# RMSNorm with every row written twice: gamma by three DMAs and one broadcast, the second load as two transfers

## The chip, the cores and the metric

The kernel runs on one core of a Trainium2 chip. The metric is device time in microseconds (us) for one execution; lower is better. The time of the kernel before is the median of three executions. The profile is one execution, recorded by the hardware profiler. In it ACT is the scalar engine, DVE the vector engine, POOL the GpSimd engine, SP the engine that issues most DMAs, and PE the matmul engine, which this kernel doesn't use.

## The reference

```python
B, S, D = 8, 512, 2048                       # x: (8, 512, 2048) float32, gamma: (2048,) float32

def reference(x, gamma):
    x_rep = np.repeat(x, 2, axis=1)
    rms = np.sqrt((x_rep ** 2).mean(axis=-1, keepdims=True) + 1e-6)
    return (x_rep / rms * gamma[None, None, :]).astype(np.float32)   # (8, 1024, 2048)
```

Each of the 4096 rows of x is divided by its root mean square, multiplied by gamma, and written twice in a row. 33.55 MB are read and 67.11 MB are written.

## The kernel before, in words

**Tiling.** The 4096 rows are taken in four loads of 1024. In one load every one of the 128 partitions gets 8 consecutive rows, 64 KB that lie together in memory. Each row is written twice, so a load makes two stores of the same size: 4 rows a partition, doubled, are 64 KB again. All the data stays in one buffer `y` of 24 rows a partition, which is used as three regions of 8 rows (L47, `first`, `second`, `third`).

**Stages.** `four(n, constants)` handles two loads, `n` and `n + 1`, and is called twice. Load `n` goes to rows 4 to 11, load `n + 1` to the region `third` (rows 16 to 23). For each group of 4 rows:

- `squares` runs on ACT: one pass a row (L63), which squares it and adds it up, and then the root of all rows of the group (L67).
- `scale` runs on DVE: the reciprocal of the roots (L73), then for each row one instruction (L75) that multiplies by it and by `gamma_b`, which has gamma in every partition.
- `repeat` copies each scaled row beside itself, on ACT or DVE (L82).
- `store` is one DMA from SP (L53).

In `four` the stores come in the order `first`, `second`, `first` again, `third`; call them store 1 to 4 of a call. The scaling for store 3 writes where store 1 reads, so it waits for store 1 to have landed.

**Order.** `manual_schedule` is on: every engine runs its instructions in the order in which the program writes them. All loads (L50) and stores (L53) are issued by SP, and so share one DMA queue, q1 in the profile. Gamma's DMAs are issued by ACT, on queue q10. SP issues both loads of a call first; then it waits in turn for what each store needs. The loads of the second call wait for stores of the first that read the same rows.

**Gamma.** `constants` is called once, between the two first loads. Gamma's first 2000 elements go as 16 pieces of 125 (500 B) into partition 0 of rows 0 and 1 of `y` (L121), with a gap after each piece; the other 48 go as three DMAs of 16 elements (64 B) into partition 0 of row 2 (L127). `y` is free there until the first scaling. Then POOL copies partition 0 to all 128 partitions of `gamma_b`, in two instructions: the 2000 elements (L131) once the first DMA has landed, and the 48 (L135) once the three have. After its DMA issues ACT loads its function table and takes one root that nothing uses (L139).

The helper that builds the program (`kernel`) is the same in both. Lines L157 and L168 of the profile belong to it.

Of the kernel before, what the change touches and what calls it, by code (L numbers as in the profile page):

```python
# [1 line left out]

# [4 lines left out]


@with_exitstack
def kernel(  # L10
    ctx: ExitStack,
    tc: tile.TileContext,
    x: bass.AP,
    gamma: bass.AP,
    out: bass.AP,
):
    nc = tc.nc
    P = nc.NUM_PARTITIONS
    f32 = mybir.dt.float32
    Act = mybir.ActivationFunctionType  # L20
    Alu = mybir.AluOpType

    B, S, D = x.shape
    Bo, So, Do = out.shape
    R = So // S
    assert R == 2 and D == Do and B == Bo and So == S * R
    eps = 1e-6
    inv_d = 1.0 / float(D)


    K = 4
    N = B * S
    ntiles = N // (P * K)
    assert N % (P * K) == 0 and ntiles == 8
    H = 2
    x_t = x.rearrange("b s d -> (b s) d").rearrange("(n p k) d -> n p k d", p=P, k=H * K)
    out_t = out.rearrange("b s d -> (b s) d").rearrange("(n p h j) d -> n h p (j d)", p=P, h=H, j=K * R)

    singles = ctx.enter_context(tc.tile_pool(name="singles", bufs=1))
    rows = ctx.enter_context(tc.tile_pool(name="rows", bufs=1))  # L40
    junk = ctx.enter_context(tc.tile_pool(name="junk", bufs=1, space=bass.MemoryType.PSUM))
    small = ctx.enter_context(tc.tile_pool(name="small", bufs=4))

    y = rows.tile([P, 3 * K * R, D], f32, name="y")
    first, second, third = 0, K * R, 2 * K * R  # L47

    def load(n, at):
        nc.sync.dma_start(out=y[:, at : at + H * K, :], in_=x_t[n])  # L50

    def store(n, h, to):
        nc.sync.dma_start(  # L53
            out=out_t[n, h], in_=y[:, to : to + K * R, :].rearrange("p j d -> p (j d)")
        )

    def squares(at, rows):

        n = len(rows)
        ss = small.tile([P, n], f32, name=f"ss{n}")  # L60
        for c, k in enumerate(rows):
            sq = junk.tile([P, D], f32, name="sq")
            nc.scalar.activation(  # L63
                out=sq[:], in_=y[:, at + k, :], func=Act.Square, accum_out=ss[:, c : c + 1]
            )
        rms = small.tile([P, n], f32, name=f"rms{n}")
        nc.scalar.activation(out=rms[:], in_=ss[:], func=Act.Sqrt, scale=inv_d, bias=eps_t[:])  # L67
        return rms

    def scale(at, to, rows, rms):  # L70
        n = len(rows)
        rstd = small.tile([P, n], f32, name=f"rstd{n}")
        nc.vector.reciprocal(out=rstd[:], in_=rms[:])  # L73
        for c, k in enumerate(rows):
            nc.vector.scalar_tensor_tensor(  # L75
                out=y[:, to + R * k, :], in0=y[:, at + k, :], scalar=rstd[:, c : c + 1],
                in1=gamma_b[:], op0=Alu.mult, op1=Alu.mult,
            )

    def repeat(to, k0, k1, copy):  # L80
        y_r = y[:, to + R * k0 : to + R * k1, :].rearrange("p (k r) d -> p k r d", r=R)
        copy(out=y_r[:, :, 1, :], in_=y_r[:, :, 0, :])  # L82

    ctx.enter_context(tc.manual_schedule())

    half = K // 2
    up, down = list(range(K)), list(range(K - 1, -1, -1))

    def four(n, constants):


        load(n, first + K)
        constants()
        load(n + 1, third)
        for rows in (up[:half], up[half:]):
            scale(first + K, first, rows, squares(first + K, rows))
        repeat(first, 0, half, nc.scalar.copy)
        repeat(first, half, K, nc.vector.tensor_copy)
        store(n, 0, first)
        scale(second, second, down, squares(second, down))  # L100
        repeat(second, half, K, nc.scalar.copy)
        repeat(second, 0, half, nc.vector.tensor_copy)
        store(n, 1, second)
        roots = [squares(third + h * K, up) for h in range(H)]
        scale(third, first, up, roots[0])
        repeat(first, 0, half, nc.scalar.copy)
        repeat(first, half, K, nc.scalar.copy)
        store(n + 1, 0, first)
        scale(third + K, third, up, roots[1])
        repeat(third, 0, K, nc.scalar.copy)  # L110
        store(n + 1, 1, third)

    gamma_b = singles.tile([P, D], f32, name="gamma_b")
    G, E = 16, 3
    C = D // G - E
    gamma_s = y[0:1, 0:2, :].rearrange("p k (c d) -> p (k c) d", c=G // 2)
    gamma_t = y[0:1, 2, :]
    eps_t = singles.tile([P, 1], f32, name="eps_t")

    def constants():  # L120
        nc.scalar.dma_start(  # L121
            out=gamma_s[0:1, :, :C],
            in_=gamma[: G * C].rearrange("(p c d) -> p c d", p=1, c=G),
        )
        for c in range(E):
            at = G * C + c * G
            nc.scalar.dma_start(  # L127
                out=gamma_t[0:1, c * G : (c + 1) * G],
                in_=gamma[at : at + G].partition_broadcast(1),
            )  # L130
        nc.gpsimd.partition_broadcast(  # L131
            out_ap=gamma_b[:, : G * C].rearrange("p (c d) -> p c d", c=G),
            in_ap=gamma_s[0:1, :, :C],
        )
        nc.gpsimd.partition_broadcast(out_ap=gamma_b[:, G * C :], in_ap=gamma_t[0:1, : E * G])  # L135
        nc.vector.memset(eps_t, eps)  # L136

        root = singles.tile([P, 1], f32, name="root")[:]
        nc.scalar.activation(out=root, in_=eps_t[:], func=Act.Sqrt)  # L139

    four(0, constants)
    four(2, lambda: None)


# [1 line left out]
_INS = ['x', 'gamma']  # L146
_OUTS = [((8, 1024, 2048), 'float32')]


# [23 lines left out]
```

## Time and profile before

| | us |
|---|---|
| time, median of 3 | 238.84 (238.44 to 238.92) |
| time of the profiled execution | 238.52 |
| span in that execution, first to last instruction | 236.3 |
| DVE busy | 84.4 |
| ACT busy | 110.2 |
| POOL busy | 2.8 |
| ACT waiting for loads, in total (2 waits) | 70.4 |
| the first load, from issue to landing | 22.0 |

The profiled execution's own time is 0.3 us under the median. It is 2.2 us longer than its span: that part lies outside the program's first and last instruction.

A row of the timeline gives the start and the length in us, the engine, the line, the operation, what it writes and reads, and in brackets how long the engine stood idle before it and what released it. An engine's name with a q (SPq, ACTq) is its sequencer, issuing a DMA: its length there is that of the issue, not of the transfer. In the page's part on DMA queues, each queue has its packets, the MB that they moved, and the time that they took as a share of 16 DMA engines over the whole span.

### The profile page before, as it was taken

Reading aid. Unit: us, or ns where it says so; the run is one execution under the profiler, and the core shown is the slowest. Engines: PE = TensorE matmul, PEld = TensorE weight load, DVE = VectorE, ACT = ScalarE, POOL = GpSimd, SP = SyncE. Lnnn points to the kernel's source line nnn. Section 1 sums busy time; section 2 is a strip of 40 time slices with the busy share of each in tenths; the row PEclk is TensorE's granted clock in tenths of the full one; section 3 lists DMA queues with packets and bytes.
Section 4 is the critical chain, followed back from the end, with each engine's and each line's share of the span. In section 5 each row is a group of like instructions: output and inputs, shape, how many; then the busy total and the mean of one; then the engine's idle time right before and its main releaser. Section 6 shows DMA issues by size and latency. Waiting matters only on the chain.

```text
span 236.3 us, 225 instructions
## 1 busy us (share of the span) xinstructions
DVE 84.4 (36%) x47; ACT 110.2 (47%) x86; POOL 2.8 (1%) x6
## 2 busy tenths in 40 slices
DVE  0000396594699500000000007929919992000000
ACT  2001989479998470000000049991999957400000
POOL 0110000000000000000000000000000000000000
DMA  9898989989898989999898988989898988989894
GB/s 355 356 532 355 521 366 466 422 388 499 355 532 356 521 366 466 422 399 488 355 532 355 510 377 377 510 355 532 355 532 355 510 377 388 499 355 532 355 532 177
DMA packets 1767, 100.68 MB, mean 426 GB/s; under 512 B 230, under 2 KB 230, under 8 KB 230
## 3 DMA queue, kind: packets, MB, share of 16 engines
q1 hardware_dynamic: 1728, 100.66, 98.7%
q10 hardware_dynamic: 38, 0.01, 0.0%
q14 instruction: 1, 0.01, 0.0%
HBM read 33.56 MB, written 67.11 MB: 426 GB/s over the span
## 4 chain that ended last, share of the span: by engine, by line
DMA 45%; ACT 26%; DVE 12%; issue 2%; DVEq 0%
DMA y<-in_x_dram 26%; DMA out_dram<-y 19%; ACT sq L63 15%; DVE y L75 12%; ACT y L82 11%; ACT rms L67 1%; DVE rstd L73 0%; DVEq L75 0%
## 5 line engine op out<-in xcount | busy, mean ns | idle before, releaser
L63 ACT ACTIVATE sq<-y 128x2048 f32<-128x2048 f32 x32 | 60.1, 1878 | 71.1 <-DMA y<-in_x_dram 70.4
L75 DVE SCALAR_TENSOR_TENSOR y<-y,rstd,gamma_b 128x2048 f32<-128x2048 f32 x32 | 73.8, 2348 | 1.6 <-DMA out_dram<-y 1.0
L82 ACT COPY y<-y 128x4096 f32<-128x4096 f32 (+1 forms) x10 | 42.6, 4283 | 19.1 <-DVE y L75 18.3
L73 DVE RECIPROCAL rstd<-rms 128x4 f32<-128x4 f32 (+1 forms) x10 | 1.7, 170 | 109.2 <-ACT rms L67 109.2
L82 DVE COPY y<-y 128x4096 f32<-128x4096 f32 x4 | 9.2, 2294 | 0.1
L63 ACT ACTIVATION_READ_ACCUMULATOR sq<-y 128x1 f32 x32 | 6.0, 186 | 0.0
L67 ACT ACTIVATE rms<-ss,eps_t 128x4 f32<-128x4 f32 (+1 forms) x10 | 3.0, 297 | 0.3
L139 ACT ACT_TABLE_LOAD x1 | 1.3, 1283 | 2.6 <-issue 2.6
L131 POOL PARTITION_BROADCAST gamma_b<-y x1 | 2.2, 2243 | 10.2 <-DMA y<-in_gamma_dram 10.2
L135 POOL PARTITION_BROADCAST gamma_b<-y x1 | 0.3, 323 | 10.2 <-DMA y<-in_gamma_dram 10.2
L136 DVE MEMSET eps_t<- 128x1 f32 x1 | 0.1, 59 | 0.8 <-PEq L157 0.8
L139 ACT ACTIVATE root<-eps_t 128x1 f32<-128x1 f32 x1 | 0.2, 202 | 0.0
L157 POOL MEMSET const-bfloat16-1.0<- 128x1 bf16 x1 | 0.1, 101 | 0.0
L157 POOL MEMSET const-uint8-127<- 128x1 uint8 x1 | 0.1, 101 | 0.0
L157 POOL MEMSET const-float32-0.0<- 128x1 f32 x1 | 0.1, 98 | 0.2 <-issue 0.2
L157 POOL MEMSET const-float32-1.0<- 128x1 f32 x1 | 0.1, 99 | 0.0
## 6 DMA issues: line engine op xcount, KB each, us to landing
out_dram<-y SPq DMA_DIRECT2D x8, 24.7
y<-in_x_dram SPq DMA_DIRECT2D x4, 31.4
y<-in_gamma_dram ACTq DMA_DIRECT2D x3, 0.1 KB
y<-in_gamma_dram ACTq DMA_DIRECT2D x1, 7.8 KB, 9.9
```

The costliest lines, as they stand in the source:

```text
L63: nc.scalar.activation(out=sq[:], in_=y[:, at + k, :], func=Act.Square, accum_out=ss[:, c : c + 1])
L67: nc.scalar.activation(out=rms[:], in_=ss[:], func=Act.Sqrt, scale=inv_d, bias=eps_t[:])
L73: nc.vector.reciprocal(out=rstd[:], in_=rms[:])
L75: nc.vector.scalar_tensor_tensor(out=y[:, to + R * k, :], in0=y[:, at + k, :], scalar=rstd[:, c : c + 1], in1=gamma_b[:], op0=Alu.mult, op ...
L82: copy(out=y_r[:, :, 1, :], in_=y_r[:, :, 0, :])
L131: nc.gpsimd.partition_broadcast(out_ap=gamma_b[:, : G * C].rearrange("p (c d) -> p c d", c=G), in_ap=gamma_s[0:1, :, :C],)
L135: nc.gpsimd.partition_broadcast(out_ap=gamma_b[:, G * C :], in_ap=gamma_t[0:1, : E * G])
L136: nc.vector.memset(eps_t, eps)
L139: nc.scalar.activation(out=root, in_=eps_t[:], func=Act.Sqrt)
L157: nc = _bacc.Bacc("TRN2", target_bir_lowering=False, num_devices=1)
```

## The change

The new `constants` loads gamma straight into partition 0 of `gamma_b`, by three DMAs from ACT. Each takes 16 pieces, one from each block of 128 elements: columns 0 to 47, 48 to 87, and 88 to 127 of every block, so pieces of 192, 160 and 160 B. One broadcast by POOL then copies partition 0 of `gamma_b` to all of its partitions, once all three have landed. The areas of `y` that held gamma are no longer used for it.

`load` can now cut a transfer by partitions. In the first call of `four` the second load becomes two DMAs on SP, partitions 0 to 63 and 64 to 127, each of 4.19 MB. The three other loads stay whole. The root is the same instruction with another way to name its tile.

```diff
-    def load(n, at):
-        nc.sync.dma_start(out=y[:, at : at + H * K, :], in_=x_t[n])
+    def load(n, at, parts=(0, P)):
+        for p0, p1 in zip(parts, parts[1:]):
+            nc.sync.dma_start(out=y[p0:p1, at : at + H * K, :], in_=x_t[n, p0:p1])
...
-    def four(n, constants):
+    def four(n, constants, ahead=(0, P)):
 
 
         load(n, first + K)
         constants()
-        load(n + 1, third)
+        load(n + 1, third, ahead)
...
-    G, E = 16, 3
-    C = D // G - E
-    gamma_s = y[0:1, 0:2, :].rearrange("p k (c d) -> p (k c) d", c=G // 2)
-    gamma_t = y[0:1, 2, :]
     eps_t = singles.tile([P, 1], f32, name="eps_t")
 
     def constants():
-        nc.scalar.dma_start(
-            out=gamma_s[0:1, :, :C],
-            in_=gamma[: G * C].rearrange("(p c d) -> p c d", p=1, c=G),
-        )
-        for c in range(E):
-            at = G * C + c * G
-            nc.scalar.dma_start(
-                out=gamma_t[0:1, c * G : (c + 1) * G],
-                in_=gamma[at : at + G].partition_broadcast(1),
-            )
-        nc.gpsimd.partition_broadcast(
-            out_ap=gamma_b[:, : G * C].rearrange("p (c d) -> p c d", c=G),
-            in_ap=gamma_s[0:1, :, :C],
-        )
-        nc.gpsimd.partition_broadcast(out_ap=gamma_b[:, G * C :], in_ap=gamma_t[0:1, : E * G])
+        G = 16
+        g_in = gamma.rearrange("(p c d) -> p c d", p=1, c=G)
+        g_to = gamma_b[0:1, :].rearrange("p (c d) -> p c d", c=G)
+        for c0, c1 in ((0, 48), (48, 88), (88, D // G)):
+            nc.scalar.dma_start(out=g_to[:, :, c0:c1], in_=g_in[:, :, c0:c1])
+        nc.gpsimd.partition_broadcast(out_ap=gamma_b[:], in_ap=gamma_b[0:1, :])
         nc.vector.memset(eps_t, eps)
...
-    four(0, constants)
+    four(0, constants, ahead=(0, P // 2, P))
     four(2, lambda: None)
```

Every instruction behind the edits stands one line further down until `constants`: what was L50, L53, L63, L67, L73, L75 and L82 is L51, L54, L64, L68, L74, L76 and L83. Gamma's DMAs are L122, its broadcast L123, the table load and the root L127.

More of the change, by code (lines that the diff above doesn't have):

```diff
@@ L113 @@
     gamma_b = singles.tile([P, D], f32, name="gamma_b")
-    G, E = 16, 3
-    C = D // G - E
-    gamma_s = y[0:1, 0:2, :].rearrange("p k (c d) -> p (k c) d", c=G // 2)
-    gamma_t = y[0:1, 2, :]
     eps_t = singles.tile([P, 1], f32, name="eps_t")
     def constants():
-        nc.scalar.dma_start(
-            out=gamma_s[0:1, :, :C],
-            in_=gamma[: G * C].rearrange("(p c d) -> p c d", p=1, c=G),
-        )
-        for c in range(E):
-            at = G * C + c * G
-            nc.scalar.dma_start(
-                out=gamma_t[0:1, c * G : (c + 1) * G],
-                in_=gamma[at : at + G].partition_broadcast(1),
-            )
-        nc.gpsimd.partition_broadcast(
-            out_ap=gamma_b[:, : G * C].rearrange("p (c d) -> p c d", c=G),
-            in_ap=gamma_s[0:1, :, :C],
-        )
-        nc.gpsimd.partition_broadcast(out_ap=gamma_b[:, G * C :], in_ap=gamma_t[0:1, : E * G])
+        G = 16
[4 more added lines that the diff above has]
+        nc.gpsimd.partition_broadcast(out_ap=gamma_b[:], in_ap=gamma_b[0:1, :])
         nc.vector.memset(eps_t, eps)
-        root = singles.tile([P, 1], f32, name="root")[:]
-        nc.scalar.activation(out=root, in_=eps_t[:], func=Act.Sqrt)
-    four(0, constants)
+        root = singles.tile([P, 1], f32, name="root")
+        nc.scalar.activation(out=root[:], in_=eps_t[:], func=Act.Sqrt)
+    four(0, constants, ahead=(0, P // 2, P))
     four(2, lambda: None)
```

## The prediction

> **What bounds the kernel now.** The page comes first: the slices, the transfer counts, the queues.
>
> ```profile
> span 236.3 us, 225 instructions
> DVE 84.4 (36%) x47; ACT 110.2 (47%) x86; POOL 2.8 (1%) x6
> ...
> DMA  9898989989898989999898988989898988989894
> ...
> q1 hardware_dynamic: 1728, 100.66, 98.7%
> q10 hardware_dynamic: 38, 0.01, 0.0%
> ```
>
> No compute engine is busy for half of the span, while the 16 DMA engines never drop under 8 tenths before the last slice. Queue q1 holds SP's four loads and eight stores; its packets alone fill 98.7% of 16 engines' span. So the kernel ends when that queue has drained.
>
> A packet's price: 12 transfers of 128 rows of 64 KB are 1536 data packets, and 16 completions each are 192 more, which gives the 1728. So 0.987 x 236.3 x 16 / 1536 = 2.43 us for 64 KB on one engine. A transfer puts 8 packets on each engine: 8 x 2.43 = 19.4 us, and twelve are 233 of the 236.3 us.
>
> Next the windows, to see whether a load is priced like a store (columns: window, length, busy of DVE, ACT, POOL, PEclk, DMA share, GB/s).
>
> ```profile
> 43.00:117.00 74.00, 30.33 (x16) 35.02 (x25) 0.00 (x0) 1.00 1.02 439
> 121.00:156.00 35.00, 11.85 (x7) 16.37 (x16) 0.00 (x0) 1.00 1.04 449
> ```
>
> The first window holds stores alone, the second loads alone. Both are full, at one rate within the rounding of 64 KB packets to a window's edges. All of this traffic spans 128 partitions.
>
> Last the timeline and the waits around gamma and the first store.
>
> ```profile
> 0.72 0.86 SPq L50 DMA_DIRECT2D y<-in_x_dram  x2
> ...
> 10.67 2.24 POOL L131 PARTITION_BROADCAST gamma_b<-y  x1 [10.25 <-DMA y<-in_gamma_dram]
> ...
> 23.07 0.32 POOL L135 PARTITION_BROADCAST gamma_b<-y  x1 [10.15 <-DMA y<-in_gamma_dram]
> ...
> 27.38 4.61 DVE L75 SCALAR_TENSOR_TENSOR y<-y,rstd,gamma_b 128x2048 f32<-128x2048 f32 x2
> ...
> 39.24 0.35 SPq L53 DMA_DIRECT2D out_dram<-y  x1
> ```
>
> gamma_b is whole at 23.07 + 0.32 = 23.39 us, 4.0 us before its first use; that use waits for the roots of the first load, not for gamma. The first store is issued at 39.24, when the second load (issued at about 1.2; 40.9 is the longest landing of a load) still has until about 42.1. Even the tightest hand-over leaves the queue covered, by 2.9 us.
>
> **The change, part by part.**
>
> *Gamma's issues on ACT.* Before, four took 0.59 + 1.21 = 1.8 us; now three, between 0.21 and 0.67 us each by the same rows, so 0.6 to 2.0. The table load and the root behind them end at 4.08 now, and ACT then waits for the first load until 22.72. That 18.64 us wait hides it: 0. Without that cover it would cost at most 0.2.
>
> *Gamma's packets.* q10's 38 are the 16 pieces of L121 and one 64 B piece of each L127 issue, each with a completion: 2 x (16 + 3). Three DMAs of 16 pieces make 96. The trace's packet records have 26 ns for 500 B and 9 ns for a completion: an engine had 35 ns, three of them (or one, three times) the 64 B pieces besides; now it has at most 3 x (26 + 9) = 105. These lie in the queue's own time: +0.07 us, bounds 0 and 0.2.
>
> *Gamma's landing and the broadcast.* The first DMA landed at 10.67, three more by 23.07, or 4.1 us apiece; two more land between 18.9 and 23.07. One broadcast is 2.24 x 2048/2000 = 2.3 us and, as POOL now waits for all three, it ends between 21.2 and 25.4. The first L75 needs it at 27.38, so at least 2.0 us are left; nothing else stands on POOL. Cost 0. Were it late by more than 2.0 + 2.9 us, store 1 would miss the queue's end.
>
> *The extra SP issue.* 0.34 to 0.43 us at about 1.6; SP next stands waiting until 39.24, and the queue holds two loads by then: 0. One completion more per engine: 0.01. ACT's squares of the second load now wait for two landings; they stand behind other work until 52.42, so a landing before that costs nothing. Behind them on ACT are only this pair's own squares and copies.
>
> *The second load itself, 128 partitions becoming 64 and 64.* This is the whole question. The pieces of L121 went to one partition and still made 16 packets, so engines are dealt out by pieces and not by partition: each half should run on all 16 engines, four packets apiece, the second half behind the first. No row shows a large transfer into 64 partitions.
> - Lower bound: each engine keeps its 2.43 us a packet. Then 4 x 2.43 twice is 19.4, as before: +0.
> - Upper bound: each partition keeps the most it is ever seen to take in. The whole is 8.39 MB in 19.4 us, 432 GB/s, or 3.4 GB/s a partition. 64 partitions then take 216 GB/s, each half 4.19 MB needs 19.4 us, and both 38.8: +19.4.
>
> What the edit halves is the number of partitions within reach at a time, so the rate per partition is the nearer row: no row has any part of the SBUF taking in more, while the lower bound asks double of it. I take +19.4.
>
> [...]
>
> *What is late next.* The load then lands at 42.1 + 19.4 = 61.5, and ACT's squares of it, at 52.42 now, wait 9 us; their first root, at 60.55 + 0.30, comes near 70. Store 1 stands behind the load on the same queue and lands near 80.8 instead of just before 61.48, where the L75 that waited for it starts. That L75, which overwrites what store 1 reads, then starts at 80.8: four of them (9.14) and the last copy of two (3.6) have store 3 issued near 93.6, and the queue reaches it, two stores of 19.4 after 61.5, at about 100. So neither delay sets the end. As the queue has no idle time to give up, nothing is won back later.
>
> *Sum.* The profiled execution took 238.52 us (span 236.3 and 2.2 around it); 238.52 + 19.4 + 0.07 + 0.01 = 258.0. It lay 0.3 under the median of 238.84, which the range covers.
>
> **The rivals.**
>
> *Half the partitions take the full rate.* Then everything but 0.1 us is hidden: 238.9. For it: every packet of the profile has one price, loads and stores alike, as if the engines alone set the rate. Against it: nothing in the profile ever put 16 engines on 64 partitions.
>
> *The halves overlap in part.* If engines drift apart, some are in the second half while others still fill the first, and both sides of the SBUF are in use. With half of the collision gone: +9.7, so 248.3. Against it: the slices show the engines in step (8 and 9 tenths throughout), and step is what makes them collide.
>
> *Faster, by the engine that ends last.* The three 64 B DMAs made one packet each, so they may all have sat on one engine and delayed it. q10's share rounds to 0.0%, below 0.05% of 16 x 236.3 us: at most 1.9 us. If all of that was on one engine, if that engine ended last, and if the halves keep the full rate, spreading gamma evenly gives up to 1.9 us back: 236.9 at best, 237.9 with half of it. It decides once the second load costs under 1 us. Against it: the records price such packets at some 10 ns.
>
> *The split is no split*, because the engines are dealt by partition after all, 8 for each half: then the halves run side by side and the time is that of the first rival.
>
> **How the numbers follow.** The forecast, 258.0, gets 0.66. Its own range is 255.5 to 260.6: one packet's overlap where the halves meet (2.43) below, and above it a fresh start for the second half, 22.0 us of the first load's landing less 19.4, so 2.6. Partial overlap 0.10, no loss 0.12 (the fourth rival within it), faster 0.12. Holding 8 in 10 needs the forecast, partial overlap and most of no loss: 238.5 to 260.6. A measurement of this kernel can tell about 0.2%, 0.48 us, from no change: faster 0.12, same 0.11, slower 0.77.
>
> **What would show it.** Queue counts of 13 x 16 + 1536 = 1744 and 96 confirm the packets. Right: the slices between 22 and 61 us move about half the GB/s at an unchanged busy share; store 1 lands near 80; ACT's wait for loads grows by about 9 us, and DVE's for stores from 1.0 to some 11; the mean falls to 394 GB/s. Wrong: five loads land with the second whole at about 42, and the span is within 1 us. gamma is wrong if its broadcast ends after 25.4, or if a DVE wait on POOL appears.

## The result, and the profile after

| | before | after |
|---|---|---|
| time, median of 5 runs each, us | 238.45 | 259.46 (259.19 to 259.65) |
| ratio to before | | 1.0871 (95%: 1.0856 to 1.0887) |
| span of the profiled execution, us | 236.3 | 257.5 |

The change costs 21.0 us; the forecast was 258.0, with 255.5 to 260.6 as its own range. The page of the changed kernel, in the lines that answer to those shown of before:

```profile
span 257.5 us, 224 instructions
DVE 84.4 (33%) x47; ACT 110.4 (43%) x86; POOL 2.5 (1%) x5
...
DMA  8979997895998998998998998998998998998995
GB/s 326 490 336 316 285 204 163 173 295 193 479 458 367 479 458 367 479 458 367 479 458 367 479 448 367 489 449 367 489 448 367 489 438 377 489 428 387 489 428 224
...
q1 hardware_dynamic: 1744, 100.66, 98.8%
q10 hardware_dynamic: 96, 0.01, 0.0%
```

DVE and ACT do the same work in the same time (DVE 84.4 us in both kernels, ACT 110.2 and 110.4), and queue q1 is as full as before: 98.8% beside 98.7%, of a longer span. The two digit rows have to be read against each other. From the fifth to the tenth slice (a slice is 257.5 / 40 = 6.4 us, so from 26 to 64 us) the GB/s fall to about half, 219 on average, while the digits of the DMA row stay at 5 to 9. (A packet counts whole in the slice in which it starts, so with long packets the digits swing.) The windows put numbers on that stretch and show DMA engines that are as busy there, a share of 1.02 beside 0.97, and move half as much; first the kernel before, then the changed one (columns: window, length, busy of DVE, ACT and POOL, PEclk, DMA share, GB/s).

```profile
25.00:60.00 35.00, 23.55 (x13) 29.06 (x26) 0.00 (x0) 1.00 0.97 419
70.00:140.00 70.00, 9.94 (x6) 14.38 (x4) 0.00 (x0) 1.00 1.00 433
```

```profile
25.00:60.00 35.00, 23.55 (x13) 22.56 (x21) 0.00 (x0) 1.00 1.02 210
70.00:140.00 70.00, 18.64 (x10) 24.47 (x15) 0.00 (x0) 1.00 1.00 434
```

In the stretch of the cut load 210 GB/s are moved instead of 419; afterwards both kernels move the same, 433 and 434. In the trace's records of single packets, nearly every 64 KB packet takes 2.42 us, and most of those of the cut load take 5.13. The first packet that an engine takes of each half is shorter: 4.3 to 5.1 us in the first half, 4.8 to 5.0 in the second. The eight of an engine add up to 40.3 us on average, where eight at 2.42 make 19.3.

The timeline shows how the rest follows (start, length, engine, line, operation, and in brackets the idle time before it with its releaser). First two rows of the kernel before, then the changed one:

```profile
52.42 1.88 ACT L63 ACTIVATE sq<-y 128x2048 f32<-128x2048 f32 x1
...
61.48 9.14 DVE L75 SCALAR_TENSOR_TENSOR y<-y,rstd,gamma_b 128x2048 f32<-128x2048 f32 x4 [0.42 <-DMA out_dram<-y]
```

```profile
20.61 2.29 POOL L123 PARTITION_BROADCAST gamma_b<-gamma_b  x1 [20.19 <-DMA gamma_b<-in_gamma_dram]
23.65 1.88 ACT L64 ACTIVATE sq<-y 128x2048 f32<-128x2048 f32 x1 [19.54 <-DMA y<-in_x_dram]
...
63.65 1.88 ACT L64 ACTIVATE sq<-y 128x2048 f32<-128x2048 f32 x1 [10.22 <-DMA y<-in_x_dram]
...
82.92 9.14 DVE L76 SCALAR_TENSOR_TENSOR y<-y,rstd,gamma_b 128x2048 f32<-128x2048 f32 x4 [10.63 <-DMA out_dram<-y]
```

gamma_b is whole at 22.9. The second load is ready for ACT at 63.65, where ACT's squares of it began at 52.42 before; and store 1, which stands behind it in the queue, lets DVE go on at 82.92 instead of 61.48: 21.4 us later. From there the whole program is shifted.

### The profile page after: what moved, and what is told of

Same layout as the page of the kernel before. It is cut to its first block, busy times and chain, and to the rows that moved or that the text cites. A ratio compares the mean times of both kernels' runs of the same rounds, so it can differ in the third digit from the quotient of the medians.

```text
span 257.5 us, 224 instructions
## 1 busy us (share of the span) xinstructions
DVE 84.4 (33%) x47; ACT 110.4 (43%) x86; POOL 2.5 (1%) x5
## 3 DMA queue, kind: packets, MB, share of 16 engines
q1 hardware_dynamic: 1744, 100.66, 98.8%
## 4 chain that ended last, share of the span: by engine, by line
DMA 59%; DVE 14%; ACT 13%; issue 1%; DVEq 0%
DMA out_dram<-y 35%; DMA y<-in_x_dram 24%; DVE y L76 14%; ACT y L83 7%; ACT sq L64 6%; ACT rms L68 0%; DVE rstd L74 0%; DVEq L76 0%
## 5 line engine op out<-in xcount | busy, mean ns | idle before, releaser
L64 ACT ACTIVATE sq<-y 128x2048 f32<-128x2048 f32 x32 | 60.1, 1878 | 82.0 <-DMA y<-in_x_dram 81.3
L76 DVE SCALAR_TENSOR_TENSOR y<-y,rstd,gamma_b 128x2048 f32<-128x2048 f32 x32 | 73.8, 2349 | 11.8 <-DMA out_dram<-y 11.2
L83 ACT COPY y<-y 128x4096 f32<-128x4096 f32 (+1 forms) x10 | 42.8, 4285 | 29.0 <-DVE y L76 29.0
L74 DVE RECIPROCAL rstd<-rms 128x4 f32<-128x4 f32 (+1 forms) x10 | 1.7, 170 | 120.3 <-ACT rms L68 120.3
L83 DVE COPY y<-y 128x4096 f32<-128x4096 f32 x4 | 9.2, 2293 | 0.1
L64 ACT ACTIVATION_READ_ACCUMULATOR sq<-y 128x1 f32 x32 | 6.0, 186 | 0.0
L68 ACT ACTIVATE rms<-ss,eps_t 128x4 f32<-128x4 f32 (+1 forms) x10 | 3.0, 296 | 0.3
L123 POOL PARTITION_BROADCAST gamma_b<-gamma_b x1 | 2.3, 2294 | 20.2 <-DMA gamma_b<-in_gamma_dram 20.2
L127 ACT ACTIVATE root<-eps_t 128x1 f32<-128x1 f32 x1 | 0.2, 203 | 0.0
```

The lines of the kernel that those rows point to most:

```text
L64: nc.scalar.activation(out=sq[:], in_=y[:, at + k, :], func=Act.Square, accum_out=ss[:, c : c + 1])
L76: nc.vector.scalar_tensor_tensor(out=y[:, to + R * k, :], in0=y[:, at + k, :], scalar=rstd[:, c : c + 1], in1=gamma_b[:], op0=Alu.mult, op ...
L123: nc.gpsimd.partition_broadcast(out_ap=gamma_b[:], in_ap=gamma_b[0:1, :])
L127: nc.scalar.activation(out=root[:], in_=eps_t[:], func=Act.Sqrt)
```

## The experiments

Each was timed against the kernel before on the same chip; the edits are against the changed kernel unless said, and `...` stands for lines left out. "Side" is used for partitions 0 to 63 and for 64 to 127.

**e1, the split alone.** Gamma stays as in the kernel before; to that kernel, only the cut load is added, with the new `load` and the new argument of `four`.

```diff
...
-        load(n + 1, third)
+        load(n + 1, third, ahead)
...
-    four(0, constants)
+    four(0, constants, ahead=(0, P // 2, P))
```

> The second load in two transfers of 64 partitions, gamma as in the kernel before. Theory (all of the loss is the split: 16 engines writing into partitions 0 to 63, then into 64 to 127): the whole loss of the changed kernel, +21.0, so 259.4 within 0.4, with the packets of this load at 5.1 us instead of 2.42. Rival (the split costs just a doubling, +19.4, and the other 1.6 us are gamma's 96 small packets and its later broadcast): 257.9.

Measured 259.31 us, ratio 1.086 (1.0844 to 1.0876). That is 20.8 above the kernel before, beside 21.0 with the new gamma too: the loss is the split's, and gamma has no part to be seen in the 1.6 us by which 21.0 is more than a doubling (19.4).

**e2, gamma alone.**

```diff
-    four(0, constants, ahead=(0, P // 2, P))
+    four(0, constants, ahead=(0, P))
```

> Gamma as in the changed kernel, the second load whole. Theory (gamma is hidden): 238.5, within 0.3 of the kernel before; the broadcast ends near 23 us, over 4 us before the first scaling. Rival (gamma's small packets or its broadcast cost what the doubling leaves over): 240.0, 1.6 us above.

Measured 238.83 us, ratio 1.0017 (0.9997 to 1.0036). The interval does not exclude a loss of some tenths of a us, nor prove one. e3 and e8 below carry the same new gamma and lie at 1.0001 and 0.9995. The rival's 240.0 (a ratio of 1.006) is excluded, and so is a gain worth the name. The broadcast runs where it was forecast:

```profile
L123 POOL PARTITION_BROADCAST gamma_b<-gamma_b x1: 2293/2293/2293, 20.4 to 20.4; - x1
```

(The columns are shortest, median and longest in ns, and first and last start.) It ends at 22.7, and the first L76 starts at 27.3.

**e3, two transfers of all partitions.** The load is cut by rows instead of partitions. The defaults of `parts` and `ahead` become `(0, H * K)` with it.

```diff
...
-            nc.sync.dma_start(out=y[p0:p1, at : at + H * K, :], in_=x_t[n, p0:p1])
+            nc.sync.dma_start(out=y[:, at + p0 : at + p1, :], in_=x_t[n, :, p0:p1])
...
-    four(0, constants, ahead=(0, P // 2, P))
+    four(0, constants, ahead=(0, K, H * K))
```

> As the changed kernel, but the second load is cut by rows: two transfers of 128 partitions and 4 rows, each of the same 4.19 MB. Theory (the loss comes from which partitions a transfer reaches): nothing lost but a few completions and 32 KB packets, 238.6 within 0.4. Rival (any second transfer on the queue restarts the engines): a part of the loss stays, from 1 us a restart up to 259.4.

Measured 238.34 us, ratio 1.0001 (0.9985 to 1.0017). One more transfer costs nothing here. So the 21 us of the changed kernel come not from a second transfer but from which partitions each one reaches: 64 of one side there, all 128 here.

**e4, the same number of partitions, elsewhere.**

```diff
-    four(0, constants, ahead=(0, P // 2, P))
+    four(0, constants, ahead=(0, P // 4, 3 * P // 4, P))
```

> As the changed kernel, but the second load is cut at partitions 32 and 96: transfers of 32, 64 and 32 partitions. Theory (the two sides are partitions 0 to 63 and 64 to 127, and a transfer inside one side runs at half): the middle one lies half on each side and keeps 2.42 us a packet, 4 x 2.42 = 9.7; the outer ones have 2 packets an engine at 5.13, 10.3 each; 30.2 together instead of 19.4, so +10.9 and 249.4. Rival (the rate goes by how many partitions a transfer has): 4 x 5.13 for the middle one and 2 x 10.3 for each outer one, 61.7 together, +42 and 281. [...]

Measured 249.29 us, ratio 1.0439 (1.042 to 1.0458): the forecast of the sides, to 0.1 us, and 32 us away from that of the numbers. Three windows of its trace lie in the three transfers, of 32, 64 and 32 partitions, the second behind an engine's first packet of the 64:

```profile
21.60:31.20 9.60, 3.25 (x3) 7.68 (x8) 1.16 (x1) 1.00 1.03 218
34.00:41.50 7.50, 5.83 (x3) 7.44 (x6) 0.00 (x0) 1.00 0.97 419
42.00:51.60 9.60, 6.79 (x4) 4.64 (x6) 0.00 (x0) 1.00 0.99 212
```

The 64 partitions from 32 to 95 take the full rate, 419 GB/s, and their packets 2.42 us each (the first one of an engine 2.7 to 3.4), while the 32 on either outside take half, 218 and 212 GB/s. (A window counts a packet where it starts, so a short one is right only within a packet for each engine.)

**e5, quarters.**

```diff
-    four(0, constants, ahead=(0, P // 2, P))
+    four(0, constants, ahead=(0, P // 4, P // 2, 3 * P // 4, P))
```

> As the changed kernel, but the second load is cut in four transfers of 32 partitions. Theory (the side decides, not the number of partitions): each has 2 packets an engine, each quarter lies within one side, so 5.13 us a packet as with 64: 8 x 5.13 = 41.1 instead of 19.4, +21.7 and 260.2. Rival (half of the partitions again means half of the rate): 8 x 10.3 = 82, +63 and 301.

Measured 259.74 us, ratio 1.0881 (1.0863 to 1.0899).

```profile
25.00:60.00 35.00, 23.55 (x13) 22.32 (x21) 0.00 (x0) 1.00 1.02 210
```

32 neighbouring partitions are fed as fast as 64 of one side, 210 GB/s in both. So there is no fixed rate for a partition: 210 GB/s over 32 are 6.6 for each, about twice the 3.4 of a load in the kernel before (432 GB/s over 128).

**e6, both halves in flight at once**, from two queues.

```diff
...
-        load(n + 1, third, ahead)
+        load(n + 1, third, ahead[:2])
...
-            scale(first + K, first, rows, squares(first + K, rows))
+            rms = squares(first + K, rows)
+            if rows[0] == 0:
+                load(n + 1, third, ahead[1:], nc.scalar)
+            scale(first + K, first, rows, rms)
```

`load` takes the issuing queue as a new argument.

> As the changed kernel, but partitions 64 to 127 of the second load are issued by ACT, behind its first two squares (about 28 us), so that from then on the engines take packets of both halves by turns. Theory A (engines that share a side stay in step, and then both take the same half at the same time): the load keeps most of its loss, 255 to 259.5. Theory B (taking turns breaks the step, so that both sides are fed): only the packets before 28 us, one or two an engine, cost double: +2.7 to +5.4, so 241 to 244.

Measured 258.37 us, ratio 1.0826 (1.081 to 1.0842): theory A.

```profile
q1 hardware_dynamic: 1664, 96.47, 91.2%
q10 hardware_dynamic: 176, 4.20, 7.6%
```

By the records of single packets the engines do take those of q1 and of q10 by turns from about 37 us on, but all 16 turn within some 1.1 us of each other, to the same side, and the packets take 4.9 to 5.1 us on either. Only the last of q10, beside packets of store 1, are down to 4.1 to 4.6. All of this wins some 1.1 us of the 21 (258.37 beside 259.46).

**e7, a store.** The loads are whole, and store 2 of the first call is cut at partition 64; `store` takes `parts` as `load` does.

```diff
...
-        store(n, 1, second)
+        store(n, 1, second, apart)
...
-    four(0, constants, ahead=(0, P // 2, P))
+    four(0, constants, ahead=(0, P), apart=(0, P // 2, P))
```

> The loads all whole; instead store 2 of the first call (region second) is cut at partition 64. Theory (the limit is that of a side of the SBUF, whichever way the data goes): half of the rate, as for the load: 8 x 5.13 instead of 8 x 2.42, +21 and 259.5. Rival (only writing into the SBUF is limited so; reading from 64 partitions goes at full rate): 238.6.

Measured 260.94 us, ratio 1.0934 (1.0917 to 1.095). Reading from one side was as slow here as writing into it: most packets take 5.12 us, beside 5.13 in the cut load, and those at the start and end of a half 3.6 to 6.3. The eight of an engine add up to 39.7 us, no more than the cut load's 40.3; so the 1.4 us that this run lies above its forecast are not in the cut store, and where they come from was not followed. A window inside the cut store:

```profile
64.00:97.00 33.00, 15.92 (x8) 19.00 (x10) 0.00 (x0) 1.00 1.08 222
```

**e8, every other partition.**

```diff
-        for p0, p1 in zip(parts, parts[1:]):
-            nc.sync.dma_start(out=y[p0:p1, at : at + H * K, :], in_=x_t[n, p0:p1])
+        step = len(parts) - 1
+        for p0 in range(step):
+            nc.sync.dma_start(out=y[p0::step, at : at + H * K, :], in_=x_t[n, p0::step])
```

> As the changed kernel, but the second load is cut into even and odd partitions: two transfers of 64, each with 32 partitions on either side of partition 64. Theory (two sides, nothing finer): both sides are fed, full rate, 238.6. Rival (the limit lies in smaller groups, and the engines' turns meet on half of these): 8 x 5.13 again, 259.4. [...]

Measured 238.35 us, ratio 0.9995 (0.9983 to 1.0008). Two transfers of 64 partitions each, and nothing is lost. Its window over the second load, beside that of the kernel before over the same stretch (first e8, then before):

```profile
23.00:41.00 18.00, 11.85 (x7) 17.09 (x16) 0.00 (x0) 1.00 0.94 408
```

```profile
23.00:41.00 18.00, 11.85 (x7) 17.08 (x16) 0.32 (x1) 1.00 0.95 411
```

By itself this looks like two sides and nothing finer, so the next one asks that directly.

**e9, eighths.**

```diff
-    four(0, constants, ahead=(0, P // 2, P))
+    four(0, constants, ahead=range(0, P + 1, P // 8))
```

> As the changed kernel, but the second load is cut in eight transfers of 16 partitions, one packet an engine each. Theory (there are finer groups than the two sides, and 16 partitions reach half as many of them as 32 do): four engines meet at each, so a packet takes twice 4.84 to 5.13, and 8 of them 77 to 82 instead of 19.4: +58 to +63, 296 to 301. Rival (two sides and nothing finer, as the quarters and the even and odd partitions would allow): 8 x 5.13 as with halves and quarters, some +22, 260. [...]

Measured 292.59 us, ratio 1.2254 (1.223 to 1.2278). The rival's 260 is excluded: 16 neighbouring partitions run at about a quarter of the full rate, 112 GB/s beside 419, and at about half of what 32 get, 210.

```profile
30.00:85.00 55.00, 23.00 (x12) 18.90 (x16) 0.00 (x0) 1.00 0.99 112
```

The size missed, by 3.4 us on the low side: a packet takes 9.22 us, less than four times 2.42 = 9.68. Groups of partitions finer than the two sides are the author's explanation of the eighths' rate; no trace shows a group, or engines that meet at one. Such groups and e8's full rate, 408 GB/s, go together if the engines, dealt out over the even partitions, do not meet at the same groups at the same time. Which engine takes which partitions there was not measured, and stays open.

**e10, the cut twice.**

```diff
-    four(2, lambda: None)
+    four(2, lambda: None, ahead=(0, P // 2, P))
```

> As the changed kernel, and the second load of the second call is cut at partition 64 as well. Theory (each cut load costs 8 packets of 5.1 instead of 2.42, and as the queue is never idle nothing takes it back): twice +21, so 280.5 within 1. Rival (part of the loss belongs to the start of the kernel, where the first load and gamma are still landing): the second cut costs less, 260 to 278.

Measured 281.09 us, ratio 1.1783 (1.1744 to 1.1822): 42.4 us above the kernel before, twice the 21. The start of the kernel has no part in it, and nothing downstream takes any of it back. Its two cut loads, in the two calls of `four`:

```profile
26.00:60.00 34.00, 23.55 (x13) 21.14 (x19) 0.00 (x0) 1.00 1.05 216
160.00:196.00 36.00, 23.55 (x13) 23.91 (x21) 0.00 (x0) 1.00 1.01 208
```

One rival was given no run of its own: that the limit lies on the side of the DRAM. In a load each partition's 64 KB follow on those of the partition before, so a cut by partitions is a cut by addresses too. Two runs speak against it. The middle 64 of e4 lie in one stretch of 4.19 MB as each half does, and run at the full rate, 419 GB/s. In e7 the 64 KB of neighbouring partitions lie 128 KB apart in the output, so the cut falls twice as far on in addresses, and costs as much: 39.7 us for an engine's eight packets, beside 40.3. No run moved the rows in the DRAM against the partitions, so this is not excluded outright.

No version ran faster than the kernel before. e3 and e8, the two cuts that lose nothing, are level with it.

## Why the prediction was right

**What bounds the kernel: right.** The queue was full before and is full after (98.7% and 98.8%), and the 21.0 us that the cut load added to it (40.3 less 19.3) were +21.0 in the result, +20.8 in e1, and +42.4 in e10, where the cut is made twice.

**Gamma: right in every term.** 96 packets and 1744 on q1 are on the page. The broadcast was to end between 21.2 and 25.4, and ended at 22.9. ACT's issues for it end before the table load at 2.62, where that stood at 2.59 before. Its packets were to cost 0.07, which is below what e2 could resolve.

**The second load: the right end of the bounds, for a reason that does not hold, and 1.6 us too small.** The upper bound was taken because "each partition keeps the most it is ever seen to take in". e5 gives each partition about twice that (6.6 GB/s beside 3.4), and e4 gives as much to the middle 64 (419 over 64, 6.5). What the runs show instead is a rate that goes by where the partitions of a transfer lie: 64 or 32 neighbouring ones of one side get 210 to 222 GB/s, 16 get 112, the 64 from 32 to 95 get 419, and every other one gets 408. A limit for each of several groups of partitions, of which a transfer must reach all at a time to run at the full rate, would fit these numbers; it is the author's explanation, and the groups were not observed. Halves of 64 give nearly the same number by both laws. That they do is luck: the number could not tell the laws apart, and the experiments did.

The size: the term was 8 x 2.43 us more, an exact halving of the rate. The packets measured 5.13 instead of 4.84, 6% beyond the doubling. Eight at 5.13 would be +21.7; the first packets of each half are shorter, and +21.0 is left (40.3 less 19.3). That they are shorter because the engines are still out of line there is likely, and was not tested. The range's upper end reached it by allowing for another cause, a fresh start of the second half; e3, which has that start and loses nothing (238.34 us), shows no such cost. That the range held is luck in that part.

**What is late next: right.** DVE's wait for stores was to be some 11 us and is 11.2; ACT's for loads was to grow by 9 and grew by 10.9 (70.4 to 81.3). The waits (total, times, longest), of the kernel before and of the changed one:

```profile
ACT sq L63 <- DMA y<-in_x_dram: 70.4, 2, 51.8
DVE y L75 <- DMA out_dram<-y: 1.0, 2, 0.6
```

```profile
ACT sq L64 <- DMA y<-in_x_dram: 81.3, 3, 51.6
DVE y L76 <- DMA out_dram<-y: 11.2, 2, 10.6
```

Neither delays the queue: store 3 is issued at 95.72, and by the records of single packets the engines go from one packet to the next without a break until then and beyond.

**The rivals.** Full rate for half of the partitions fell with the result. Partial overlap, by engines that drift apart, did not happen, and even turns between two queues (e6) hardly make it happen, with 1.1 us won of 21: the engines stay in step. The prediction read that from the slices of 8 and 9 tenths, which show engines that are busy, not engines in step; the single packets of the changed kernel show it, as an engine's second one in the cut load begins between 26.0 and 27.7 us on all 16 of them. That step is what makes them collide is argued, not shown: no run had them far out of step. A faster end by a more even gamma was not seen (e2). Engines dealt out by partition would have run the halves side by side at full rate; the 5.13 us packets exclude that.

## What to carry to other kernels

When a kernel is bound by its DMA queue, look at which partitions each transfer reaches before you look at how many transfers there are: two transfers of 128 partitions, or of every other one, cost nothing here (238.34 and 238.35 us), and one cut at partition 64 cost 21 us. In the profile of the changed kernel this stands where the DMA share stays full (1.02) and the GB/s halve (210 beside 419); the share alone does not show it. And where two bounds lie far apart, ask which other layout would separate the laws behind them: the middle 64 partitions did it in one run.

## What the runs showed of the hardware

- The slowdown does not go by clean doublings. A packet of 65,536 B takes 2.42 us in a load of all partitions, 5.13 in the halves (5.12 in those of e7's store) and 9.22 in the eighths, so an engine moves 27.1, 12.8 and 7.1 GB/s. The first step is 2.12 times and the second 1.80, 3.81 together. Why was not tried.
- The landing of a whole load was felt later where a transfer to few neighbouring partitions followed it on the queue: ACT's first squares start at 22.64 to 22.72 where the next one is whole, cut by rows or by every other partition (e2, e3, e8), at 23.07 in e1 and 23.65 in the changed kernel, where a half follows, and at 24.93 in e9, where an eighth does (one profile each). In the changed kernel it cost nothing: store 1 is issued at 40.21, and the queue reaches it at about 62 (61.6 to 63.0 over the engines).
- The store cut at partition 64 was held up as the cut load was (e7: 5.12 us a packet and 222 GB/s, beside 5.13 and 210), though it only reads from the SBUF.
